# Turning the attention maps on VectorE and through DRAM instead of on TensorE, with a new order of TensorE's and GpSimd's work

## The chip, the cores and the metric

The kernel runs on one core of one Trainium2 chip. A core has TensorE (matrix products into the eight PSUM banks), VectorE, ScalarE and GpSimd, each with an instruction queue of its own that is worked through in the order in which it was written, and SyncE, which here only issues DMAs. GpSimd's queue issues DMAs too. The metric is the device time of one execution in microseconds (us); the median of three runs stands for a kernel.

## The reference

Two layers over 256 tokens of width 1024. In each layer the normalised input goes through one large projection, whose columns feed a gated DeltaNet branch and a differential attention branch. Cut to what the change touches:

```python
def attend(q_blk):                      # one head: two maps of 256 x 256
    s = jnp.einsum('nbhqd,nbhkd->nbhqk', q_blk, k).astype(f32)
    p = jax.nn.softmax(s, axis=-1)
    a = p[0] - lam * p[1]
    return jnp.einsum('bhqk,bhkd->bhqd', a.astype(v.dtype), v)
...
o = rmsnorm(o, subln_w) * (1.0 - lambda_init)
return o * jax.nn.silu(z)               # z: zb below
...
merged = (jax.nn.sigmoid(gate_a) * (y_a @ w_pa[l]) + jax.nn.sigmoid(gate_b) * (y_b @ w_pb[l]))
x = x + merged @ w_out[l]
```

There are eight heads of attention. The DeltaNet branch (the other eight heads) needs for each head and direction the inverse of a triangular matrix; the kernel inverts 32x32 blocks by substitution on VectorE and merges them into 64 and then 128 on TensorE.

## The kernel before

**Projections.** A projection of 512 columns contracts over 1024 rows in eight slices of 128 (`kt`). Each slice is six products on TensorE (two blocks of 128 tokens, three terms each, L324 to L326), since weights and activations are split into a high and a low part. I call these six products a step. Weights come in pairs of slices: SyncE loads `raw` (512 KB), ScalarE makes `hi` (L308), VectorE makes `lo = raw - hi` (L310). `hi` and `lo` have two buffers each, so a pair can be prepared only when TensorE is done with the pair two before it.

**Numbering.** From the projection `zb0` on, steps are counted from 0: `zb0` is 0 to 7, `zb1` 8 to 15, `za0` 16 to 23, `za1` 24 to 31, `gb0` 32 to 39, `gb1` 40 to 47, `ga0` 48 to 55, `ga1` 56 to 63, then `pb`. Everything else that TensorE does in this stage is put between steps.

**Attention, one head.** `scores` (L1053): four products `sc` per head (eight instructions in the trace, since a product of f32 is two), maxima on VectorE (`mx`, L1069), exponentials on ScalarE (`es`, L1071), the factor `cc` and the difference of the two maps on VectorE (L1074 to L1077). `turn` (L1081): four transposes `at` on TensorE into PSUM (L1088) and a copy to `aT` on ScalarE (L1090). `attend` (L1093): four products `av` with `vb` (L1099), a copy to `ob` and two sums of squares on ScalarE. The maps `es` and the turned maps `aT` have two buffers each.

**Inverse.** `substitute` (L865) runs 31 short pairs of VectorE instructions on `X` (L870, L871), spread over the projections until `za1`. `spread_blocks` (L873) copies `X` turned into `lt` and stores both to DRAM as `udr` on GpSimd's queue (L878). `merges` loads them back as `T` (L905; for the first group of heads by GpSimd's queue, for the second by SyncE's) and `U` (L909, GpSimd's queue), and then works in turns: `y64p` at step 41, `zt` at 43 and 45, `y128p` at 48, the next `zt` at 50. `weigh_q` needs products `kq` at 39, 42, 44 and 47. `chunks` follows from step 52 on.

**After attention.** The sums of squares `ssb` of all heads go to `rb` (VectorE, then a power on GpSimd, L155 and L156), `rb` scales `ob` (L1191, sixteen instructions), and `send` and `fetch` turn the result by the way that the change now uses for the maps: a transpose on VectorE inside blocks of 32x32 (L249), a store to DRAM on GpSimd's queue (L251), and four loads of 32 partitions each that put the blocks in their places (L257). The turned tile has its elements four apart in memory, and ScalarE and VectorE read it so (`split_B`, L263 and L265). The tiles `tb_v` of the DeltaNet branch go the same way (L135, L140, L142).

**What sets the order.** A scheduler orders the instructions of each engine by its own estimates; `behind(x)` (`tc.issue_after`) puts an instruction behind `x` in its engine's queue, and `keep_in_program_order` does so for the written order. Before the change only the first instructions of some groups are tied to a step (`place`); the rest is the scheduler's choice.

Of the kernel before, what the change touches and what calls it, by code (L numbers as in the profile page):

```python
# [17 lines left out]
P = 128  # L18
# [31 lines left out]
def hybrid_encoder(  # L50
# [53 lines left out]
    mark = {}  # L104
# [53 lines left out]
    def norm_row(w_row, nm):  # L158
# [14 lines left out]
        for i in range(3):  # L173
            mm = T.matmul(wb[i > 0], one if i else tri[:, 0, :], hl[:, i - 1] if i else row,
                          start=i < 2, stop=i != 1)
            tc.keep_in_program_order(mm)
# [138 lines left out]
    def proj_tm(act, w, c0, n, evac, nm, places=(None,) * 4, spare=(), later=None, turned=(), between=None,  # L315
# [3 lines left out]
        for kt, hi, lo in weights(w, c0, n, nm, places, later=later, spare=spare, turned=turned, held=held,  # L319
                                  first=first, raws=raws):  # L320
            for m in range(NM):
                ts_ = slice(m * P, (m + 1) * P)
                o = accs[m][:, :n]
                T.matmul(o, act[kt // 4][:, 0, kt % 4, ts_], hi, start=kt == 0, stop=False)  # L324
                T.matmul(o, act[kt // 4][:, 0, kt % 4, ts_], lo, start=False, stop=False)  # L325
                mark["proj"] = T.matmul(o, act[kt // 4][:, 1, kt % 4, ts_], hi, start=False,  # L326
                                        stop=kt == KT - 1).ins
                mark["done", nm, kt] = mark["proj"]
        if between:
            between()  # L330
        for m in range(NM):
            evac(m, accs[m][:, :n])
# [76 lines left out]
    for _ in range(5):  # L409
        mm = T.matmul(idle[:, :P], ones, ones, start=True, stop=True)  # L410
        tc.keep_in_program_order(mm)
# [22 lines left out]
    for m in range(NM):  # L434
        mm = T.matmul(pos_p[:, m : m + 1], pos_r[:, m * P : (m + 1) * P], ones[0:1, 0:1], start=True, stop=True)
        mark["pos"] = mm.ins
        tc.keep_in_program_order(mm)
# [69 lines left out]
    for l in range(DEPTH):  # L507
# [86 lines left out]
        def qk_part(s_, i):  # L594
                def evac_qk(m, ps):
# [11 lines left out]
                    for b in range(4):  # L607
# [4 lines left out]
                proj_tm(hT, wl, (C_QB, C_KB)[s_] + 512 * i, 512, evac_qk, f"qk{l}{s_}{i}",  # L612
                        turned=(0, 1) if (s_, i) == (0, 1) else ())
# [170 lines left out]
        def gram(nm, g, c, slot, after=None):  # L784
            gp = (bank if slot else bank_c)(f"{nm}{l}{g}{c}")
            for j4 in range(4):
                kqh = kq[:, 4 * g + j4, c]
                with behind(after):
                    mark[nm, g, c] = T.matmul(gp[:, j4 * P : (j4 + 1) * P], kqh[:, 0, :], kqh[:, slot, :],
                                              start=True, stop=True).ins  # L790
# [35 lines left out]
        def weigh_q(g, c, after):  # L826
            bv = B[:, c, 4 * g : 4 * g + 4]
            with tc.high_priority(offset=HP):
                gp = gram("kq", g, c, 1, after)
# [67 lines left out]
        def merges(g):  # L897
# [3 lines left out]
            G.memset(T64[blk(0), 0:8, 32:64], 0.0)  # L901
# [482 lines left out]
```

## Time and profile before

| | |
|---|---|
| time, median of three runs | 749.93 us (749.83 to 750.06) |
| span of the profiled execution | 748.5 us; the runs' median is 1.4 us longer, which lies around the span |
| busy | TensorE 739.3 us (99%), VectorE 586.5 (78%), ScalarE 481.2 (64%), GpSimd 139.5 (19%) |
| mean DMA rate | 181 GB/s |

A row of the groups gives line, engine, operation, output<-inputs, count, busy time and the mean of one in ns, then the idle time of the engine just ahead of it. A row of the timeline gives start, duration and what ran. Back to back instructions overlap in the trace, so what an instruction takes of its engine is read from start to start and not from its duration. "Issue" as a releaser means that nothing in the profile shows what was waited for.

### The profile page before, as it was taken

How to read it: one execution, taken by the hardware profiler on the slowest of the kernel's cores; microseconds unless marked ns; L12 is line 12 of the kernel's file. 1: busy time of each engine (PE TensorE's matmuls, PEld its weight loads, DVE VectorE, ACT ScalarE, POOL GpSimd, SP SyncE). 2: the span in 40 equal slices, each digit the busy share in tenths (PEclk: the TensorE clock that was granted, in tenths of full speed). 3: DMA queues.
4: the chain of work that ended last, by engine and by line, in shares of the span. 5: the costliest groups of instructions: out<-in, count | busy, mean ns of one | idle time of the engine just before them, and what ended most of it. 6: DMA issues, size and time to landing. Idle time of an engine off the chain costs nothing.

```text
span 748.5 us, 13917 instructions
## 1 busy us (share of the span) xinstructions
PE 739.3 (99%) x5176; PEld 641.7 (86%) x5176; DVE 586.5 (78%) x1109; ACT 481.2 (64%) x1022; POOL 139.5 (19%) x221
## 2 busy tenths in 40 slices
PE   8999999999999999999999999999999999999996
PEld 6999889987888889888889899889778888998885
DVE  8696898999985965578668779999999679537782
ACT  6757875667876576645456578555687757566552
POOL 6004110112023440100000150202110425301000
PEclk9999999999999999999999999999999999999999
DMA  8754566776667462567674466767666748335641
GB/s 260 239 170 169 170 179 198 209 211 193 208 177 186 145 184 84 171 200 247 199 232 133 128 192 180 219 176 230 195 171 195 197 133 229 95 114 201 220 141 57
DMA packets 73734, 135.46 MB, mean 181 GB/s; under 512 B 12944, under 2 KB 13921, under 8 KB 73666
## 3 DMA queue, kind: packets, MB, share of 16 engines
q1 hardware_dynamic: 64750, 113.65, 50.6%
q0 software_dynamic: 7936, 19.35, 8.7%
q10 hardware_dynamic: 980, 1.58, 0.6%
q8 instruction: 41, 0.67, 0.4%
q14 instruction: 27, 0.22, 0.1%
HBM read 125.53 MB, written 9.01 MB: 180 GB/s over the span
## 4 chain that ended last, share of the span: by engine, by line
PE 95%; ACT 2%; issue 1%; DVE 1%; DMA 1%; SPq 0%; POOLq 0%; POOL 0%; DVEq 0%; ACTq 0%
PE pp_vb L369 4%; PE pp_qk L325 4%; PE pp_qk L326 3%; PE pp_qk L324 3%; PE sc L1061 2%; PE pp_o L369 2%; PE pf_k L385 2%; PE pp_za L325 2%; PE pf_v L385 2%; PE pf_v L389 2%; PE pp_gb L324 2%; PE pp_gb L325 2%; PE pp_zb L324 2%; PE pf_q L387 2%; PE pf_k L387 2%; PE pf_v L387 2%
## 5 line engine op out<-in xcount | busy, mean ns | idle before, releaser
L325 PE MATMUL pp_qk<-lo_qk,hT 128*128 128x512 f32 x128 | 50.5, 395 | 0.3
L326 PE MATMUL pp_qk<-hi_qk,hT 128*128 128x512 f32 x128 | 50.0, 390 | 0.0
L310 DVE TENSOR_TENSOR lo_qk<-raw_qk,hi_qk 128x1024 fp32r<-128x1024 f32 x32 | 39.1, 1222 | 11.6 <-ACT hi_qk L308 11.4
L324 PE MATMUL pp_qk<-hi_qk,hT 128*128 128x512 f32 x128 | 45.1, 393 | 0.0
L308 ACT CAST hi_qk<-raw_qk 128x1024 fp32r<-128x1024 f32 x28 | 29.4, 1049 | 23.4 <-PE pp_qk L326 12.4
L1071 ACT ACTIVATE es<-sc,mx 128x256 f32<-128x256 f32 x64 | 29.6, 474 | 19.5 <-DVE mx L1069 19.5
L387 PE MATMUL pf_q<-hT,hi_q 128*128 128x256 f32 x128 | 36.1, 286 | 0.0
L385 PE MATMUL pf_k<-hT,hi_k 128*128 128x256 f32 x128 | 36.1, 287 | 0.0
L385 PE MATMUL pf_v<-hT,hi_v 128*128 128x256 f32 x128 | 35.9, 285 | 0.0
L387 PE MATMUL pf_v<-hT,hi_v 128*128 128x256 f32 x128 | 35.8, 284 | 0.0
L385 PE MATMUL pf_q<-hT,hi_q 128*128 128x256 f32 x128 | 35.8, 284 | 0.0
L387 PE MATMUL pf_k<-hT,hi_k 128*128 128x256 f32 x128 | 35.8, 284 | 0.0
L310 DVE TENSOR_TENSOR lo_pb<-raw_pb,hi_pb 128x1024 fp32r<-128x1024 f32 x16 | 19.6, 1225 | 20.5 <-ACT hi_pb L308 20.2
L389 PE MATMUL pf_q<-hT,lo_q 128*128 128x256 f32 x128 | 35.2, 288 | 0.0
L389 PE MATMUL pf_v<-hT,lo_v 128*128 128x256 f32 x128 | 34.6, 288 | 0.0
L389 PE MATMUL pf_k<-hT,lo_k 128*128 128x256 f32 x128 | 34.3, 284 | 0.0
L308 ACT CAST hi_pa<-raw_pa 128x1024 fp32r<-128x1024 f32 x16 | 16.8, 1053 | 22.3 <-PE pp_pa L326 16.1
L679 DVE SCALAR_TENSOR_TENSOR cvq<-pf_q,cw,cvq 128x254 f32<-128x254 f32 (+1 forms) x64 | 30.0, 479 | 0.9 <-ACT cvq L675 0.3
L679 DVE SCALAR_TENSOR_TENSOR cvv<-pf_v,cw,cvv 128x254 f32<-128x254 f32 (+1 forms) x64 | 30.1, 482 | 0.1
L679 DVE SCALAR_TENSOR_TENSOR cvk<-pf_k,cw,cvk 128x254 f32<-128x254 f32 (+1 forms) x64 | 29.0, 478 | 1.3 <-ACT cvk L675 0.6
L325 PEld LDWEIGHTS pp_qk<-lo_qk,hT 128*128 128x128 f32 x128 | 24.0, 188 | 6.6 <-DVE lo_qk L310 1.6
L310 DVE TENSOR_TENSOR lo_pa<-raw_pa,hi_pa 128x1024 fp32r<-128x1024 f32 x16 | 19.6, 1224 | 11.1 <-ACT hi_pa L308 11.1
(414 smaller groups left out, 2542.2 us busy)
## 6 DMA issues: line engine op xcount, KB each, us to landing
raw_qk<-in_w_in_dram SPq DMA_DIRECT2D x32, 512.0 KB, 3.8
raw_k<-in_w_in_dram SPq DMA_DIRECT2D x16, 512.0 KB, 4.7
raw_q<-in_w_in_dram SPq DMA_DIRECT2D x16, 512.0 KB, 3.7
raw_v<-in_w_in_dram SPq DMA_DIRECT2D x16, 512.0 KB, 3.8
raw_zb<-in_w_in_dram SPq DMA_DIRECT2D x16, 512.0 KB, 3.7
raw_za<-in_w_in_dram SPq DMA_DIRECT2D x16, 512.0 KB, 3.7
raw_ga<-in_w_in_dram SPq DMA_DIRECT2D x16, 512.0 KB, 4.4
raw_pb<-in_w_pb_dram SPq DMA_DIRECT2D x16, 512.0 KB, 3.8
```

The costliest lines, as they stand in the source:

```text
L308: high = (V.tensor_copy if kp in turned else S.copy)(hi[:, :, :n], raw[:, :, :n]).ins
L310: mark[nm, kp] = high, V.tensor_tensor(lo[:, :, :n], raw[:, :, :n], hi[:, :, :n].bitcast(F32), ALU.subtract).ins
L324: T.matmul(o, act[kt // 4][:, 0, kt % 4, ts_], hi, start=kt == 0, stop=False)
L325: T.matmul(o, act[kt // 4][:, 0, kt % 4, ts_], lo, start=False, stop=False)
L326: mark["proj"] = T.matmul(o, act[kt // 4][:, 1, kt % 4, ts_], hi, start=False, stop=kt == KT - 1).ins
L369: mark["proj"] = T.matmul(o, act[kt // 4][:, pa, kt % 4, ts_], ws[kt][1 + pw], start=kt == 0 and n_ == 0, stop=kt == KT - 1 and n_ == 2).ins
L385: T.matmul(o, hi[:, cs], act[kt // 4][:, 0, kt % 4, :], start=first, stop=False, skip_group_check=True)
L387: T.matmul(o, hi[:, cs], act[kt // 4][:, 1, kt % 4, :], start=False, stop=False, skip_group_check=True)
L389: T.matmul(o, lo[:, cs], act[kt // 4][:, 0, kt % 4, :], start=False, stop=done, skip_group_check=True)
L679: V.scalar_tensor_tensor(ca[:, o0:o1], acc[:, b, o0 + sft : o1 + sft], cw[:, j, cb : cb + 1], ca[:, o0:o1], ALU.mult, ALU.add)
L1061: mm = T.matmul(sp[n][:, qt * SEQ : (qt + 1) * SEQ], qkT[h // 4][rows, 0, h % 4, qt * P : (qt + 1) * P], qkT[h // 4][rows, 1, h % 4, :], s ...
L1071: S.activation(es[:, n, qt, :], spv[:, qt, :], AF.Exp, bias=mx[:, n, qt : qt + 1], accum_out=s_all[:, h, n, qt : qt + 1])
```

## The change

**TensorE's order is written out.** Each product of the projections, of attention and of the merges now goes through `mm`, which ties it behind the one before it. The chain begins at `zb0` and ends after `pb`. Projections became generators; `drive` takes a step and then runs the jobs that `plan` has put there.

**Places.** Scores come after steps 3, 8, 13, 18, 23, 28, 33, 37; the products with v after 14, 19, 24, 29, 34, 39, 44, 46. Before, scores began after 3, 7 and 12 and then every four steps, and the products with v followed some three steps later; the last were put after 39.

**Turning.** The four transposes on TensorE, the PSUM bank and ScalarE's copy go. VectorE transposes the blocks of the map into the free half of `es`, GpSimd's queue stores it as `att` and loads it back with four DMAs. The product reads its stationary operand with elements four apart (16 bytes).

**GpSimd's queue.** Loads of turned maps are kept in order by `mark["queued"]`. The clearing of `T` and its loads are tied behind the loads of head 5's map, the loads of `U` behind those of head 6's, and head 7's map behind `U`.

```diff
+    def mm(*args, **kw):
+        if mark["chain"] is None:
+            return T.matmul(*args, **kw)
+        with behind(mark["chain"]):
+            made = T.matmul(*args, **kw)
+        mark["chain"] = made.ins
+        return made
...
-            G.memset(T64[blk(0), 0:8, 32:64], 0.0)
-            G.memset(T64[blk(3), 8:16, 0:32], 0.0)
+            with behind(mark["queued"]):
+                G.memset(T64[blk(0), 0:8, 32:64], 0.0)
+                G.memset(T64[blk(3), 8:16, 0:32], 0.0)
             for b in range(4):
...
             for b in range(4 if g == 0 else 0):
-                G.dma_start(out=U_[blk(b), :, :, blk(b)].rearrange("j g t i -> j (g t) i"),
-                                  in_=udr[0, b].rearrange("g t j i -> j (g t) i"))
+                with behind(mark["queued"]):
+                    mark["queued"] = G.dma_start(out=U_[blk(b), :, :, blk(b)].rearrange("j g t i -> j (g t) i"),
+                                                 in_=udr[0, b].rearrange("g t j i -> j (g t) i")).ins
...
-                            mark["at", h] = T.transpose(ap_[:, kt * SEQ + qt * P : kt * SEQ + (qt + 1) * P],
-                                                        es[:, 0, qt, kt * P : (kt + 1) * P], ident).ins
-                S.copy(aT.rearrange("p k q -> p (k q)"), ap_)
...
+            V.transpose(es[:, 1].rearrange("p q k -> p (q k)").rearrange("p (b t x) -> p b x t", b=4, x=4),
+                        es[:, 0].rearrange("p q k -> p (q k)").rearrange("p (x b t) -> p b x t", b=4, x=4))
+            dd = dram.tile([4, 32, 4, P], F32, tag="att", name=f"att{l}{h}", bufs=4)
+            with behind(mark.get("queued")):
+                G.dma_start(out=dd.rearrange("i t j x -> (i t) (j x)"), in_=es[:, 1].rearrange("p q k -> p (q k)"))
+            back = work.tile([P, 4, 32, 4], F32, tag="w2a", name=f"aT{l}{h}", bufs=2)
+            for j in range(4):
+                with behind(mark.get("queued")):
+                    mark["queued"] = G.dma_start(out=back[blk(j)].rearrange("t i x k -> t i (x k)"),
+                                                 in_=dd[:, :, j].rearrange("i t x -> t i x")).ins
...
+            av = aT[h].rearrange("p i t x -> p x (i t)")
             for qt in range(NM):
                 for kt in range(NM):
...
+                    mm(op_[:, qt * P : (qt + 1) * P], av[:, 2 * qt + kt],
...
+        for h in range(NH):
+            plan((3, 8, 13, 18, 23, 28, 33, 37)[h], attention, h)
+        for h in range(NH):
+            plan((14, 19, 24, 29, 34, 39, 44, 46)[h], attend, h)
```

**What moves, on VectorE in `zb1`.** The rows stand between the difference of head 0's maps (`es`) and the low half of the third weight pair of `zb1`, steps 12 and 13 (`lo_zb_2210` before, `lo_zb_2211` after). Before:

```order
L1077 SCALAR_TENSOR_TENSOR es_2106<-es_2106,cc_2120 128x256 x2
L310 TENSOR_TENSOR lo_zb_2192<-raw_zb_2193,hi_zb_2191 128x1024
L1069 TENSOR_REDUCE mx_2126<-sc_2128 128x2
L399 SCALAR_TENSOR_TENSOR zb_0_385<-zb_0_385,pp_zb_2029 128x512
L1069 TENSOR_REDUCE mx_2126<-sc_2127 128x2
L871 TENSOR_TENSOR X_377<-X_377,fstmp_378 128x15x17
L690 SCALAR_TENSOR_TENSOR thv_1893<-thv_1893,cvv_1896 128x256
L310 TENSOR_TENSOR lo_zb_2210<-raw_zb_2211,hi_zb_2209 128x1024
```

The same piece of VectorE's queue after the change:

```order
L1074 SCALAR_TENSOR_TENSOR es_2066<-es_2066,cc_2080 128x256 x2
L321 TENSOR_TENSOR lo_zb_2193<-raw_zb_2194,hi_zb_2192 128x1024
L410 SCALAR_TENSOR_TENSOR zb_0_385<-zb_0_385,pp_zb_2029 128x512
L879 TENSOR_TENSOR X_377<-X_377,fstmp_378 128x15x17
L700 SCALAR_TENSOR_TENSOR thv_1893<-thv_1893,cvv_1896 128x256
L1082 STREAM_TRANSPOSE es_2066<-es_2066 128x4x4x32
L1066 TENSOR_REDUCE mx_2160<-sc_2162 128x2
L1066 TENSOR_REDUCE mx_2160<-sc_2161 128x2
L878 TENSOR_TENSOR fstmp_378<-la_375,X_377 128x256
L147 STREAM_TRANSPOSE tb_v_1904<-thv_1893 128x512
L321 TENSOR_TENSOR lo_zb_2211<-raw_zb_2212,hi_zb_2210 128x1024
```

The new transpose, a short instruction on `X` and the transpose of `tb_v` now stand ahead of that low half.

**What moves, on GpSimd's queue.** The rows run from the store of the inverted blocks (`udr`) to the loads of `T` and `U`. Before:

```order
L878 DMA udr_374<-X_377 8x8x1024 x2
L878 DMA udr_374<-lt_376 8x8x1024 x2
L909 DMA U__96<-udr_374 32x32x32 x4
L901 MEMSET T_2654 32x8x32
L902 MEMSET T_2654 32x8x32
L905 DMA T_2654<-udr_374 32x16x32 x4
```

After, with the maps of heads 5 and 6 (`att_2531` and `att_2649`) between them:

```order
L886 DMA udr_374<-X_377 8x8x1024 x2
L886 DMA udr_374<-lt_376 8x8x1024 x2
L1086 DMA att_2531<-es_2511 128x512
L1090 DMA aT_2533<-att_2531 32x4x128 x4
L910 MEMSET T_2591 32x8x32
L911 MEMSET T_2591 32x8x32
L915 DMA T_2591<-udr_374 32x16x32 x4
L910 MEMSET T_2598 32x8x32
L911 MEMSET T_2598 32x8x32
L1086 DMA att_2649<-es_2629 128x512
L1090 DMA aT_2651<-att_2649 32x4x128 x4
L920 DMA U__96<-udr_374 32x32x32 x4
```

`U` now stands behind two maps' ways through DRAM and behind `T`; just ahead of these rows stand the store and the loads of head 4's map, and head 7's follow.

**What moves, on VectorE ahead of `ga0`'s third weight pair.** That pair serves steps 52 and 53 (`lo_ga_2935` before, `lo_ga_3223` after). Before, half of the scaling of `ob` and its transposes is spread between the weight pairs ahead of it:

```order
L1233 SCALAR_TENSOR_TENSOR rb_2865<-rb_2865,r_2863 128x16
L1191 SCALAR_TENSOR_TENSOR ob_0_383<-ob_0_383,rb_2865,zb_0_385 128x128 x8
L249 STREAM_TRANSPOSE zb_0_385<-ob_0_383 128x4x4x32 x2
L830 TENSOR_TENSOR B_371<-kq_2849,B_371 128x1024
L310 TENSOR_TENSOR lo_ga_2899<-raw_ga_2900,hi_ga_2898 128x1024
L998 TENSOR_TENSOR ktm_360<-ktm_360,kds_372 128x512 x2
L1191 SCALAR_TENSOR_TENSOR ob_1_384<-ob_1_384,rb_2865,zb_1_386 128x128 x4
```

After, `rb` comes later, and all of the scaling stands in one piece ahead of the third pair:

```order
L321 TENSOR_TENSOR lo_ga_3145<-raw_ga_3146,hi_ga_3144 128x1024
L1000 TENSOR_TENSOR ktm_360<-ktm_360,kds_372 128x512 x2
L1233 SCALAR_TENSOR_TENSOR rb_3057<-rb_3057,r_3055 128x16
L1197 SCALAR_TENSOR_TENSOR ob_0_383<-ob_0_383,rb_3057,zb_0_385 128x128 x8
L147 STREAM_TRANSPOSE tb_q_3200<-kq_359 128x512
L1197 SCALAR_TENSOR_TENSOR ob_1_384<-ob_1_384,rb_3057,zb_1_386 128x128 x8
L260 STREAM_TRANSPOSE zb_0_385<-ob_0_383 128x4x4x32 x2
L321 TENSOR_TENSOR lo_ga_3223<-raw_ga_3224,hi_ga_3222 128x1024
```

The third pair's low half now follows `rb`, and through it the last product with v, which moved from step 39 to step 46.

More of the change, by code (lines that the diff above doesn't have):

```diff
@@ L313, in weights, with proj_tm @@
                 yield 2 * kp + k, hi[:, k, :n], lo[:, k, :n]
[L315 removed]
+    def proj_tm(act, w, c0, n, evac, nm, places=(None,) * 4, spare=(), later=None, turned=(),
                 banks=None, held=None, first=(), raws={}):
@@ L1279, in hybrid_encoder @@
             gated(osb, za, ro, nw[:, 0:1], yaT, f"ya{l}", (m,))
-        branch(yaT, w_pa[l], gta, f"pa{l}")
+        for i in range(2):
+            full(branch(yaT, w_pa[l], gta, f"pa{l}", i))
         mT = pair(f"mT{l}")
```

262 lines of the change are left out of this document (120 added, 142 removed).

## Prediction, made before the changed kernel ran

> **What bounds the kernel now.** I read the busy shares first, then the chain that ended last, then the stretches of the stage that changes, then its timeline engine by engine.
>
> ```profile
> PE 739.3 (99%) x5176; PEld 641.7 (86%) x5176; DVE 586.5 (78%) x1109; ACT 481.2 (64%) x1022; POOL 139.5 (19%) x221
> PE 95%; ACT 2%; issue 1%; DVE 1%; DMA 1%; SPq 0%; POOLq 0%; POOL 0%; DVEq 0%; ACTq 0%
> core 0: us, PE busy (x) PEld busy (x) DVE busy (x) ACT busy (x) POOL busy (x), PEclk, DMA share, GB/s
> 158.00:214.00 56.00, 56.00 (x296) 44.63 (x295) 54.04 (x121) 43.31 (x116) 6.41 (x12) 1.00 0.63 187
> 214.00:262.00 48.00, 48.00 (x607) 39.93 (x606) 36.33 (x61) 30.56 (x73) 17.56 (x28) 1.00 0.63 177
> 524.00:580.00 56.00, 56.00 (x296) 44.64 (x295) 54.02 (x121) 43.33 (x116) 6.45 (x12) 1.00 0.63 187
> ```
>
> TensorE is the bound: 95% of the chain is its own work, so an instruction less on it is time, if nothing else arrives late. The stretches say where something may. In layer 0 the first six heads of attention lie in 158 to 214 us, and there VectorE is busy for 54.04 of 56.00 us; layer 1 (524 to 580) has the same picture. VectorE has 2 us to spare just where the change gives it more work. After 214 it has 12 of 48 us.
>
> **What goes.** Here is TensorE around the transposes of one head, with the products of a projection behind:
>
> ```profile
> 199.99 0.60 PE L1088 MATMUL at<-ident,es 128*128 128x128 f32 x4
> 200.51 1.13 PE L1061 MATMUL sc<-qkT 64*128 64x256 f32 x8
> 202.61 0.39 PE L324 MATMUL pp_za<-hi_za,hT 128*128 128x512 f32 x1
> 202.84 0.39 PE L325 MATMUL pp_za<-lo_za,hT 128*128 128x512 f32 x1
> ...
> 205.26 0.48 PE L325 MATMUL pp_za<-lo_za,hT 128*128 128x512 f32 x1
> 205.57 0.40 PE L326 MATMUL pp_za<-hi_za,hT 128*128 128x512 f32 x1
> L1090 ACT COPY aT<-at 128x512 f32<-128x512 f32 x16 | 9.4, 585 | 0.0
> ```
>
> Four transposes take 200.51 - 199.99 = 0.52 us. Eight heads: 4.2 us a layer. The written order also has about three places fewer at which TensorE goes from f32 back to a projection, and the first product there takes 205.57 - 205.26 = 0.31 us instead of 0.23, so some 0.1 us each: 0.3 us. **Term A: -4.5 us a layer.** ScalarE's 16 copies (9.4 us) go too; ScalarE is at 43 of 56 us in the tight stretch and TensorE does not wait for it there, so I count them at nothing. A projection's product takes 0.23 us from start to start (202.61 to 202.84), so a step is 1.37 us.
>
> **What comes.** The transpose on VectorE is like `send`'s, and the way through DRAM like that of `tb_v`:
>
> ```profile
> 247.87 2.01 DVE L249 STREAM_TRANSPOSE zb<-ob 128x512 f32<-128x512 f32 x2
> 249.72 1.21 DVE L830 TENSOR_TENSOR B<-kq,B 128x1024 f32<-128x1024 f32 x1
> 180.50 0.71 DVE L135 STREAM_TRANSPOSE tb_v<-thv 128x512 f32<-128x512 f32 x1
> 181.50 0.56 POOL L140 DMA_DIRECT2D bnc_v<-tb_v  x1 [8.44 <-DVE tb_v L135]
> 185.33 2.17 POOL L142 DMA_DIRECT2D tb_v<-bnc_v  x4 [3.26 <-issue]
> DMA to landing us min/median/max: 2.1/3.3/5.7
> ```
>
> A transpose takes (249.72 - 247.87) / 2 = 0.93 us of VectorE. The store starts 0.3 us after the transpose ends (181.21 to 181.50), the loads 3.8 us after the store; the last of the four starts 1.6 us later and lands after 3.3, the median of this way's DMAs. So a map is there 0.3 + 3.8 + 1.6 + 3.3 = 9.0 us after its transpose.
>
> **Term B: head 0 to the merges.** Head 0 first. Up to the row at 175.35 VectorE's queue is the same as before.
>
> ```profile
> 172.66 1.06 PE sc L1061 x8
> 175.35 1.24 DVE L310 TENSOR_TENSOR lo_zb<-raw_zb,hi_zb 128x1024 fp32r<-128x1024 f32 x1
> 177.09 0.70 DVE L399 SCALAR_TENSOR_TENSOR zb<-zb,pp_zb 128x512 f32<-128x512 f32 x1
> 178.28 0.44 DVE L871 TENSOR_TENSOR X<-X,fstmp 128x255 f32<-128x255 f32 x1
> 178.62 0.44 DVE L690 SCALAR_TENSOR_TENSOR thv<-thv,cvv 128x256 f32<-128x256 f32 x1
> ```
>
> From 175.35 the new queue has `lo` (1.14 from start to start), the `zb` product (0.60), `X` (0.34), `thv` (0.33) and then the transpose: it ends at 178.7. Plus 9.0 gives 187.7 for the map. TensorE's old start of head 1's scores is 172.66; the new order puts them one step later (174.0), then come 1.1 us of scores, steps 9 to 13, head 2's scores and step 14: 174.0 + 1.1 + 6 x 1.37 + 1.1 + 0.3 for the changes of kind = 184.7. TensorE would wait 3.0 us at step 14, part of it already at step 12, whose low half now stands behind two transposes and two maxima. Two more low halves stand behind a map's transpose (steps 18 and 22, where no transposes of TensorE fill the time any more), up to 0.93 each: 1.9. Sum 4.9.
>
> A second way to the same lateness goes by GpSimd's queue to `U`, needed at step 43:
>
> ```profile
> 205.12 0.88 DVE L1077 SCALAR_TENSOR_TENSOR es<-es,cc 128x256 f32<-128x256 f32 x2
> 213.05 1.27 POOL L878 DMA_DIRECT2D udr<-X  x2 [25.55 <-issue]
> 222.79 3.15 POOL L909 DMA_DIRECT2D U__96<-udr  x4 [7.37 <-issue]
> 226.57 2.57 POOL L905 DMA_DIRECT2D T<-udr  x4
> 245.59 0.72 PE L937 MATMUL zt<-U__96,y 32*32 32x32 f32 x62
> ```
>
> Head 4's map was ready at 206.0; with five transposes ahead on a full engine it is turned at 206.0 + 5 x 0.93 = 210.7. Store and loads: 0.3 + 3.8 + 2.2, so `udr` is stored from 217.0 instead of 213.05. Its landing took 222.79 - 213.05 = 9.7 us: 226.7. Then `T` (2.6) with the clearing ahead of it (0.6, from the end of `U`'s row to `T`'s start), head 6's map (3.8 + 2.2), `U` (3.15, landing after 4.1 by its median): 226.7 + 3.2 + 6.0 + 2.4 + 4.1 = 242.4. TensorE without any wait would reach `zt` at 245.59 - 4.5 - 2 x 0.89 (two products with v that come later) = 239.3. Lateness 3.1. The two ways are not added: the first delays TensorE, and `U` is then in time. Bounds for B: 3.1, the second way alone, and 6.9 (VectorE's 2 us of idle time left as they are, on top of 4.9). I take **B: +4.9 us a layer**, near the first way.
>
> **Term C: `ga0`'s third weight pair (step 52).** The new queue has all of `ob`'s scaling ahead of it, and `rb` waits for head 7.
>
> ```profile
> 242.69 0.89 PE kq L789 x8
> 240.10 1.46 PE L923 MATMUL y64p<-T,A 32*32 32x32 f32 x128
> 245.55 0.18 DVE L1233 SCALAR_TENSOR_TENSOR rb<-rb,r 128x16 f32<-128x16 f32 x1 [0.71 <-POOL rb L156]
> 245.76 2.19 DVE L1191 SCALAR_TENSOR_TENSOR ob<-ob,rb,zb 128x128 f32<-128x128 f32 x8
> 257.27 2.13 PE L960 MATMUL y128p<-T,A 64*64 64x64 f32 x64
> L1207 ACT ACTIVATE gb<-pp_gb 128x512 f32<-128x512 f32 x8 | 4.8, 596 | 0.1
> ```
>
> Before, head 7's product ended at about 240.1 (`y64p` follows it) and `rb` ran at 245.55, 5.4 us later. From there now: 0.2, eight scalings 2.1, a transpose of `tb_q` 0.6 (adjacent elements, as in `tb_v`'s row less the overlap), eight more 2.1, two transposes 1.9, the low half 1.2, and 0.6 for a `gb` evacuation that ScalarE has between: 14.1. TensorE goes from head 7 (step 46) to step 52's second product through five steps (6.8), `kq` 0.9, `y128p` and `zt`, as many instructions, 2.1 each, and 0.6 besides: 12.5. **C: +1.6 us a layer**; bounds 0, if the pieces overlap, and 3.
>
> **Sum.** -4.5 + 4.9 + 1.6 = +2.0 a layer, +4.0 for both. The span of 748.5 becomes 752.5; the runs' median of 749.93 lies 1.4 above the span: 753.9.
>
> **The unknown price: a strided stationary operand.** The product with v reads `aT` with elements 16 bytes apart. No TensorE instruction of before does. ScalarE does:
>
> ```profile
> L263 ACT ACTIVATE ybT<-zb,nw 128x512 fp32r<-128x512 f32 x8 | 9.9, 1241 | 0.0
> L244 ACT ACTIVATE yaT<-pt_ya,nw 128x512 fp32r<-128x512 f32 x8 | 5.1, 682 | 0.0
> L1088 PEld LDWEIGHTS at<-ident,es x64: 138/139/146, 176.7 to 598.5; 128*128 128x128 f32 x64
> L1099 PEld LDWEIGHTS av<-vb,aT x128: 187/192/193, 179.9 to 605.5; 128*128 128x128 f32 x128
> 196.52 0.89 PE av L1099 x8
> ```
>
> The same operation takes 1241 instead of 682 ns with its input four elements apart: 1.09 ns more an element. On 128 columns that is 0.14 us a load, and with the 128 loads of the `av` row 17.9 us. The other bound is 0. I take 0, because TensorE loads 128 columns of `at` in 139 ns and those of `av` in 192 (minimum, median and maximum are given): the load of `av` is not limited by how fast a column can be read, which leaves a stride 0.05 us of slack, and the 0.11 us of the product before (0.89 us for eight) run beside it. Together that is more than 0.14.
>
> [...]
>
> **The rivals.**
>
> *Strided loads are dear.* Term D of up to +17.9, half of it if the load hides in part. Delays of the first six products also give `U` and the low halves time, so I take 12: 753.9 + 12 = 766. For it: ScalarE's rows. Against: the slack and the overlap.
>
> *TensorE's waits are hidden.* This one ends faster. Its place is VectorE between step 9 and the store of `udr`. The 2 us of idle time there and a landing at the minimum (2.1 instead of 3.3) cover 3.2 of B's 4.9, and C falls to 0. With B at 1.7: -2.8 a layer, 749.9 - 5.6 = 744. It decides where B and C together fall below 4.5. Against it: the queue's order is fixed, and 3.0 of B comes from a sum in which VectorE never waits. With nothing late at all the time would be 749.9 - 9.0 = 741.
>
> *A draw.* B and C equal A within 0.7 us a layer: 748.5 to 751.4.
>
> *The change does not do what it says*: the order of TensorE's queue shows the transposes gone and the places as written, so I give this no chance.
>
> **How the numbers follow.** Forecast (waits of 5 to 11 us a layer, cheap loads) 0.50, from 751.5 to 762; strided loads dear 0.17 (760 to 772); hidden 0.23 (741 to 748.4); draw 0.10. The range leaves out 0.1 on either side: 743 to 767. About 0.2%, 1.5 us, is what a measurement can tell from no change: faster 0.23, same 0.12 (the draw and the forecast's lower edge), slower 0.65.
>
> **What would show it.** Right: the groups have no L1088; the stretch from 158 us on shows VectorE above 95%; `av` of head 0 shows TensorE idle for about 3 us until a load of `aT`; the pair at steps 52 and 53 has TensorE waiting for `lo_ga`. Wrong: TensorE without idle time there (B, C), or the 16 groups of `av` longer than 0.89 us each (D). A landing far from 3.3 us, or `att` held behind `udr` in the queue, would upset B the most.

## The result and the profile after

The changed kernel takes **780.96 us** (778.67 to 782.83) against 749.93: a ratio of 1.041, with the 95% interval 1.0389 to 1.043. The profiled execution has a span of 781.1 us (before 748.5), so there are 32.6 us to explain. The forecast had 4.0.

Busy shares and the chain of the changed kernel:

```profile
PE 754.6 (97%) x5112; PEld 651.6 (83%) x5112; DVE 603.0 (77%) x1125; ACT 475.2 (61%) x1006; POOL 183.2 (23%) x301
PE 56%; DVE 5%; issue 3%; DMA 2%; ACT 1%; POOL 0%; POOLq 0%; DVEq 0%; ACTq 0%
```

TensorE runs 64 instructions less than before and is busy 15.3 us longer: the work that stayed became slower. And it is no longer busy throughout, so it also waits. (How much, the chain can't say: its shares add up to 67%, so it wasn't followed through a third of the span.) First the waits of TensorE (who, for what, us in total, times, longest); before, this view had nothing of this stage:

```profile
PE pp_zb L110 <- DVE lo_zb L321: 4.0, 2, 2.0
PE pp_ga L110 <- DVE lo_ga L321: 3.0, 2, 1.5
PE zt L110 <- DMA U__96<-udr: 2.9, 1, 2.9
PE av L110 <- issue: 2.7, 1, 2.7
PE pp_za L110 <- DVE lo_za L321: 2.7, 3, 1.0
PE av L110 <- DMA aT<-att: 2.6, 1, 2.6
```

They sum to 17.9 us, nearly all at places that the forecast named: low halves behind a map's transpose, the first product with v, `U`, and `ga0`'s third pair. Only the low half of step 28 (0.83 us in each layer, two of the three waits for `lo_za`) is not among them. The second source is in TensorE's timeline (start, duration, what; in brackets what it waited for):

```profile
179.37 0.61 PE L110 MATMUL pp_zb<-hi_zb,hT 128*128 128x512 f32 x2
181.99 0.50 PE L110 MATMUL pp_zb<-lo_zb,hT 128*128 128x512 f32 x1 [2.00 <-DVE lo_zb L321]
...
187.03 0.39 PE L110 MATMUL pp_zb<-hi_zb,hT 128*128 128x512 f32 x1
190.15 2.10 PE L110 MATMUL av<-vb,aT 128*128 128x128 f32 x8 [2.73 <-issue]
192.01 0.65 PE L110 MATMUL pp_zb<-hi_zb,hT 128*128 128x512 f32 x1
192.46 0.63 PE L110 MATMUL pp_zb<-lo_zb,hT 128*128 128x512 f32 x1
192.89 1.05 PE L110 MATMUL pp_zb<-hi_zb,hT 128*128 128x512 f32 x2
...
201.91 1.91 PE L110 MATMUL av<-vb,aT 128*128 128x128 f32 x8
203.57 0.48 PE L110 MATMUL pp_za<-hi_za,hT 128*128 128x512 f32 x1
```

Head 1's eight products, which wait for nothing, take 203.57 - 201.91 = 1.66 us. Their loads in the view of the tile `av` (minimum, median and maximum in ns; before 187/192/193):

```profile
L110 PEld LDWEIGHTS av<-vb,aT x128: 308/329/332, 190.1 to 649.6; 128*128 128x128 f32 x128
```

A third source shows in the same rows: from 192.46 to 192.89 one product of a projection takes 0.43 us instead of 0.23. The stretches of 3.41 us around it have the granted clock in the column behind the five engines, with the DMA share next to it:

```profile
188.74:192.16 3.42, 2.01 (x9) 2.04 (x10) 1.82 (x6) 0.68 (x4) 0.11 (x1) 1.00 0.80 261
192.16:195.57 3.41, 3.41 (x10) 2.63 (x10) 1.95 (x6) 2.88 (x9) 2.07 (x4) 0.50 0.27 78
195.57:198.98 3.41, 3.41 (x16) 2.68 (x15) 3.24 (x5) 3.24 (x9) 0.56 (x1) 1.00 0.15 49
257.01:263.84 6.83, 6.27 (x107) 5.63 (x108) 0.00 (x0) 2.25 (x6) 2.18 (x4) 0.50 0.18 53
```

Behind its three longest waits, those of 2.6 to 2.9 us, TensorE runs at half clock for one or two such stretches; behind the two of 2.0 us it does not. Besides the two stretches shown there is 577.86 to 581.28, behind layer 1's wait for head 0's map: 13.65 us in all, of which at most half, 6.8, is lost.

### The profile page after: what moved, and what is told of

The parts are those of the page before. It is cut to its first block, busy times and chain, and to the rows that moved or that the text cites. A ratio compares the mean times of both kernels' runs of the same rounds, so it can differ in the third digit from the quotient of the medians.

```text
span 781.1 us, 13961 instructions
## 1 busy us (share of the span) xinstructions
PE 754.6 (97%) x5112; PEld 651.6 (83%) x5112; DVE 603.0 (77%) x1125; ACT 475.2 (61%) x1006; POOL 183.2 (23%) x301
## 4 chain that ended last, share of the span: by engine, by line
PE 56%; DVE 5%; issue 3%; DMA 2%; ACT 1%; POOL 0%; POOLq 0%; DVEq 0%; ACTq 0%
PE pp_pb L110 6%; PE pp_pa L108 6%; PE pp_ga L110 4%; PE pp_gb L110 4%; PE pp_qk L108 4%; PE pp_vb L380 3%; PE pp_o L108 3%; PE pp_za L110 2%; PE av L110 2%; PE pp_o L380 2%; PE po L110 2%; DVE ob L1197 1%; PE pf_k L396 1%; PE pf_v L396 1%; PE pf_v L400 1%
## 5 line engine op out<-in xcount | busy, mean ns | idle before, releaser
L108 PEld LDWEIGHTS pp_qk<-hi_qk,hT 128*128 128x128 f32 x256 | 47.4, 188 | 9.1
L321 DVE TENSOR_TENSOR lo_qk<-raw_qk,hi_qk 128x1024 fp32r<-128x1024 f32 x32 | 39.1, 1221 | 10.9 <-ACT hi_qk L319 10.6
L1090 POOL DMA_DIRECT2D aT<-att x64 | 35.1, 556 | 52.4 <-PE sc L110 10.0
L110 PE MATMUL pp_ga<-hi_ga,hT 128*128 128x512 f32 x128 | 45.8, 408 | 0.0
L110 PE MATMUL pp_za<-hi_za,hT 128*128 128x512 f32 x128 | 43.8, 405 | 0.0
L110 PE MATMUL pp_zb<-hi_zb,hT 128*128 128x512 f32 x128 | 43.7, 410 | 0.0
L110 PE MATMUL pp_pb<-hi_pb,ybT 128*128 128x512 f32 x128 | 42.7, 399 | 0.0
L110 PE MATMUL pp_gb<-hi_gb,hT 128*128 128x512 f32 x112 | 40.2, 414 | 0.0
L108 PE MATMUL pp_pa<-hi_pa,yaT 128*128 128x512 f32 x128 | 39.8, 389 | 0.0
L110 PEld LDWEIGHTS av<-vb,aT 128*128 128x128 f32 x128 | 31.2, 325 | 6.8 <-issue 6.1
L110 PE MATMUL av<-vb,aT 128*128 128x128 f32 x128 | 31.0, 387 | 5.3 <-issue 2.7
```

The source lines that it names most:

```text
L108: return T.matmul(*args, **kw)
L110: made = T.matmul(*args, **kw)
L321: mark[nm, kp] = high, V.tensor_tensor(lo[:, :, :n], raw[:, :, :n], hi[:, :, :n].bitcast(F32), ALU.subtract).ins
L1090: mark["queued"] = G.dma_start(out=back[blk(j)].rearrange("t i x k -> t i (x k)"), in_=dd[:, :, j].rearrange("i t x -> t i x")).ins
```

## The experiments

Each changes the changed kernel, unless it says that it changes the kernel before; none leaves work out. Ratios are to the kernel before, run on the same chip.

### The step of 16 bytes alone

The kernel before, with one edit: ScalarE's copy writes `aT` with elements four apart, and the product reads it so. Order and ways stay.

```diff
-                S.copy(aT.rearrange("p k q -> p (k q)"), ap_)
+                S.copy(aT.rearrange("p k q -> p (k q)").rearrange("p (t x) -> p x t", x=4),
+                       ap_.rearrange("p (x t) -> p x t", x=4))
...
-                            T.matmul(op_[...], aT[:, kt, qt * P : (qt + 1) * P],
+                            T.matmul(op_[...], aT.rearrange("p k q -> p (k q)").rearrange("p (t x) -> p x t", x=4)[:, 2 * kt + qt],
```

> The kernel before, its order unchanged, but ScalarE's copy writes the turned map with elements 16 bytes apart and the product with v reads it so. Theory A, the step costs TensorE 325 - 192 = 133 ns a load, of which the product before hides a little, as in the changed kernel: 0.77 us for eight, 12.3 us in all, 762 us, and no waits. Theory B, in the changed kernel the loads were slow because transfers or VectorE used the same memory at that time: here they stay at 192 ns and the time is 750 us.

Measured: 763.80 us (763.4 to 763.85), ratio 1.0179 (1.0164 to 1.0194): +13.6 us over 750.24. The loads of `av` and one group of eight in the timeline:

```profile
L1100 PEld LDWEIGHTS av<-vb,aT x128: 308/329/332, 179.4 to 618.6; 128*128 128x128 f32 x128
```

```profile
197.56 1.91 PE L1100 MATMUL av<-vb,aT 128*128 128x128 f32 x8
199.22 0.48 PE L325 MATMUL pp_za<-lo_za,hT 128*128 128x512 f32 x1
```

The loads show the changed kernel's 329 ns, no wait of this stage appears, and the eight products take 1.66 us (before 0.81, from 196.35 to 197.16). 0.85 x 16 groups = 13.6, which is the whole difference. A load grew by 329 - 192 = 137 ns and each product by 0.85 / 8 = 106 ns, so some 30 ns of a load's growth are hidden and the rest is on TensorE's path.

**How far apart is too far?** The same edit with 8 bytes instead of 16 (`"p (k t x) -> p k x t", k=2, x=2`, and the product reads two apart):

> As e3_step_alone, but with elements 8 bytes apart in place of 16. Theory A, a load pays for each 16 bytes that it touches: 8 bytes apart costs half of what 16 does or nothing, a load of 192 to 260 ns and 750 to 757 us. Theory B, any step other than adjacent costs the whole: 329 ns and 763.8 us.

```profile
L1100 PEld LDWEIGHTS av<-vb,aT x128: 193/196/198, 180.0 to 606.5; 128*128 128x128 f32 x128
```

Measured: 751.20 us (750.69 to 752.76), ratio 1.0015 (1.0006 to 1.0024), +0.9. With elements 8 bytes apart the load is back at 196 ns.

### The order alone

The changed kernel's order, with the transposes and ScalarE's copy back on TensorE and ScalarE (after steps 12, 17, 22, 27, 32, 36, 43 and 45), no way through DRAM, and `T` and `U` not tied.

```diff
+            ap_ = bank(f"at{l}{h}")
+            back = work.tile([P, 4, P], F32, tag="w2a", name=f"aT{l}{h}", bufs=2)
...
+                        mark["chain"] = T.transpose(ap_[:, (2 * qt + kt) * P : (2 * qt + kt + 1) * P], es[:, 0, qt, kt * P : (kt + 1) * P], ident).ins
+            S.copy(back.rearrange("p x q -> p (x q)"), ap_)
...
+            plan((12, 17, 22, 27, 32, 36, 43, 45)[h], lambda h: turn(h, es[h]), h)
```

> The changed kernel's order of TensorE (scores at steps 3, 8, 13 and so on, products with v at 14, 19 and so on, merges and chunks as they stand), but the maps turned by TensorE and copied by ScalarE as before the change, one or two steps ahead of the product with v; no transpose on VectorE, no store, no map loads, and nothing to tie GpSimd's queue behind. Theory A, the waits come from VectorE's transposes and the way through DRAM: no wait for a map or for `U`, loads of 192 ns, and with some 0.1 us a head for one more change of kind the time is 750 to 753 us. Theory B, the new order by itself brings the waits for low halves and for `ob`'s scaling: 1 to 2 us each at steps 12, 18, 22 and 52, 755 to 762 us.

Measured: 759.59 us (758.85 to 761.15), ratio 1.0126 (1.0109 to 1.0143). Its waits:

```profile
PE pp_ga L110 <- DVE lo_ga L321: 3.0, 2, 1.5
PE pp_zb L110 <- DVE lo_zb L321: 2.2, 2, 1.1
PE pp_za L110 <- DVE lo_za L321: 0.6, 2, 0.3
```

The order is dear without any way through DRAM: the span is 9.0 longer than before's, 5.8 of it waits. The other 3.2 are not idle time. They can't all be charged to the changed kernel's order: the transposes stand at places of their own here, so that from `zb0` to `pb` TensorE leaves the projections 47 times a layer (40 before, 41 in the changed kernel). The wait for `lo_zb` fell from 2.0 to 1.1 each: 0.9 of it was the map's block transpose; the rest is left with the short instruction on `X` and `tb_v`'s transpose (0.97 us together, 179.13 to 180.10), which the order alone puts ahead of that low half.

### The waits, one at a time

**Head 0's and head 1's products with v later**, after steps 17 and 21 instead of 14 and 19, since a map lands 11.4 us after its transpose:

```diff
-            plan((14, 19, 24, 29, 34, 39, 44, 46)[h], attend, h)
+            plan((17, 21, 24, 29, 34, 39, 44, 46)[h], attend, h)
```

> The changed kernel with the products with v of heads 0 and 1 at steps 17 and 21 in place of 14 and 19; nothing else is moved. Theory A, the waits of 2.7 and 2.6 us of head 0's product are the time that a map needs through DRAM, and the stretches of half clock behind them (3.4 us from 192.16 and from 577.86) follow from these waits: both waits and both stretches go, 5.3 us and about 2 x 1.7 us, 772 to 773 us. Theory B, VectorE is the bound there: TensorE runs into the low halves of steps 14 to 22 that much earlier and waits for them instead, and the time is 776 to 781 us.

Measured: 770.20 us (767.86 to 771.96), ratio 1.026 (1.0243 to 1.0278). The waits at `av` and those for `lo_za` are gone and the one at `U` falls to 1.6, which leaves 8.6 us of waits: 9.3 less, and the span is 10.9 shorter. The half clock did not go (the granted clock over the span is 0.991, in the changed kernel 0.990); in layer 0 it moved behind the wait of 2.0 us for `lo_zb`, at which the changed kernel kept its full clock. First this run, then the changed kernel at the same wait:

```profile
179.77:183.19 3.42, 1.42 (x7) 1.13 (x7) 3.42 (x6) 3.42 (x11) 1.51 (x4) 1.00 0.55 170
183.19:186.60 3.41, 3.41 (x11) 2.29 (x11) 3.32 (x9) 0.80 (x2) 3.41 (x7) 0.50 0.90 275
```

```profile
178.50:181.92 3.42, 1.49 (x7) 0.91 (x5) 3.42 (x7) 2.60 (x9) 1.12 (x2) 1.00 0.53 199
181.92:185.33 3.41, 3.34 (x17) 2.57 (x19) 3.41 (x11) 1.96 (x6) 2.73 (x5) 1.00 0.89 258
```

The bounds of these stretches run on in steps of 3.41 us. Here the whole wait lay within one of them (1.42 us busy, 2.00 idle); in the changed kernel all but 0.07 us of it did (1.49 busy, 1.93 idle), and the clock held.

**`U` first.** `T` and `U` ahead of the store and loads of head 5's map, whose product moves from 39 to 42:

```diff
+            if h != 5:
+                send_map(h)
...
+        plan(32, step, mg)
+        plan(32, send_map, 5)
```

> The changed kernel with head 5's store and loads put behind the loads of `T` and `U` in GpSimd's queue in place of ahead of them, and its product with v at step 42 in place of 39. Theory A, `U` is late in layer 0 (2.86 us, and 6.8 us of half clock around it) because head 5's loads wait for a buffer that head 3's product with v frees at 235.6, and hold the queue: the wait for `U` and that half clock go, 5 to 6 us, 775 to 776 us. Theory B, `U` is late because `udr` is stored and lands late: TensorE still waits 2 us or more for `U` or `T`, or now for head 5's map, and the time is 779 to 783 us.

Measured: 778.16 us (777.74 to 778.76), ratio 1.0378 (1.0362 to 1.0393). The wait at `zt` is gone and the granted clock is 0.994 instead of 0.990, as the theory that GpSimd's queue holds `U` says. But 5 to 6 us were to go and 2.8 went (4.8 in the spans): the waits for `lo_za` grew from 2.7 to 4.0 and those for `lo_zb` from 4.0 to 4.4. What held the queue in the changed kernel shows in GpSimd's timeline:

```profile
229.60 0.61 POOL L1086 DMA_DIRECT2D att<-es  x1 [2.44 <-DVE za L410]
235.87 2.20 POOL L1090 DMA_DIRECT2D aT<-att  x4 [5.67 <-PE av L110]
...
249.25 2.34 POOL L920 DMA_DIRECT2D U__96<-udr  x3 [1.17 <-issue]
```

Head 5's loads need the `aT` buffer of head 3, which is free only after that head's product (step 29). They stand 5.67 us at the head of the queue, and everything for `T` and `U` stands behind them.

**Less on VectorE.** Three low halves to GpSimd:

```diff
-                    mark[nm, kp] = high, V.tensor_tensor(lo[:, :, :n], raw[:, :, :n],
+                    mark[nm, kp] = high, (G if (nm[:2] + nm[3:], kp) in (("zb1", 2), ("za0", 3), ("za1", 2)) else V).tensor_tensor(lo[:, :, :n], raw[:, :, :n],
```

> The changed kernel with the low halves of three weight pairs a layer (zb1's third, za0's fourth, za1's third: those that TensorE waited 2.0, 1.0 and 0.8 us for) made by GpSimd in place of VectorE. Theory A, VectorE has too much to do from 160 to 215 us, some 3.6 us a layer: with 3 x 1.14 us less the waits for low halves fall from 3.9 us in layer 0 and 2.8 in layer 1 to under 1 each, and 775 to 777 us follow if the wait for the first map stays. Theory B, a subtraction on GpSimd takes well over 2 us and slows VectorE beside it, and GpSimd's queue is held from its stores: the waits stay or grow, 780 to 788 us.

Measured: 790.80 us (787.06 to 794.14), ratio 1.0544 (1.0509 to 1.058): worse. GpSimd's timeline:

```profile
180.06 2.38 POOL L321 TENSOR_TENSOR lo_zb<-raw_zb,hi_zb 128x1024 fp32r<-128x1024 f32 x1 [5.33 <-ACT hi_zb L319]
182.39 0.58 POOL L1086 DMA_DIRECT2D att<-es  x1
```

The store of head 0's map starts at 182.39 instead of 179.35. The waits for low halves fell from 6.7 to 4.3 us, those at `av` rose from 5.3 to 16.0 (9.8 for `aT`, 6.2 for `tb_v`). So GpSimd, whose queue issues the maps' DMAs, was no free engine here.

### Both causes, taken away together

**The order mended, the step kept.** Scores of head 1 one step earlier, VectorE's transposes of heads 0 to 4 each tied behind a low half, products with v at 20, 23, 26, 30, 36, 42, 44 and 46, `T` and `U` ahead of head 5's loads, and the second half of `ob`'s scaling behind `ga0`'s third low half.

```diff
+            with behind(mark[low[h][0], low[h][1]][1] if h in low else None):
+              V.transpose(es[:, 1]...
...
+        low = {0: (f"zb{l}1", 2), 1: (f"zb{l}1", 3), 2: (f"za{l}0", 1), 3: (f"za{l}0", 3), 4: (f"za{l}1", 2)}
+            plan((12, 14, 18, 22, 28, 32, 36, 39)[h], lambda h: turn(h, es[h]), h)
+            plan((20, 23, 26, 30, 36, 42, 44, 46)[h], attend, h)
...
+            at = [mark[f"ga{l}0", 2][1] if i else mark[f"gb{l}1", 2 + m][1] for m in range(NM)]
```

> As e7_all, but the map keeps the changed kernel's way: one store of 256 KB, four loads with runs of 512 bytes, and the product with v reads elements 16 bytes apart; head 5's store may run ahead of `U`, the last two scores stand at 33 and 37. Theory A, e7_all was late only because its stores in runs of 128 bytes and its single load take 5 to 6 us each to land: here the waits for maps and low halves are under 3 us in all, no half clock follows, and what is left beside the kernel before is the step (+13.7), the transposes (-7.2) and some changes of kind (+2): 757 to 760 us. Theory B, VectorE's surplus shows up whatever the way of the map: 10 us of waits or more, 766 to 775 us.

Measured: 763.94 us (762.96 to 765.86), ratio 1.0186 (1.0172 to 1.02). What is left of waits in this stage:

```profile
PE av L110 <- DMA aT<-att: 2.6, 3, 1.4
PE pp_za L110 <- DVE lo_za L321: 1.9, 2, 0.9
PE pp_zb L110 <- DVE lo_zb L321: 0.9, 2, 0.6
...
PE pp_zb L110 <- DVE cvv L689: 0.6, 1, 0.6
```

No wait is over 1.4 us, and no stretch of this stage has half clock (the granted clock is 1.00 from 158 to 214 us and from 524 to 580, and 0.999 over the span). 17.0 us came back with the order alone, and what remains is the time of the kernel before with nothing but the step (763.80; in spans 764.1 against 761.7). So what the change saves on TensorE is spent by the 6.0 us of waits that are left, and the step comes on top.

**The step taken away too.** VectorE transposes into adjacent places; a map then goes by four stores with runs of 512 bytes, instead of one store with runs of 2 KB, and by four loads with runs of 128 instead of 512 bytes. First with the changed kernel's order:

```diff
-            dd = dram.tile([4, 32, 4, P], F32, tag="att", name=f"att{l}{h}", bufs=4)
+            dd = dram.tile([4, 4, 32, P], F32, tag="att", name=f"att{l}{h}", bufs=4)
+            for i in range(4):
...
+                    G.dma_start(out=dd[i].rearrange("j t x -> t j x"), in_=es[blk(i), 1]...)
...
+                    mark["queued"] = G.dma_start(out=back[:, :, i], in_=dd[i].rearrange("j t (x r) -> (j t) x r", x=4)).ins
-            av = aT[h].rearrange("p i t x -> p x (i t)")
+            av = aT[h].rearrange("p x i r -> p x (i r)")
```

> The changed kernel, but the map comes back with each stationary block's 128 elements side by side: VectorE writes its blocks adjacent, four stores of 64 KB in place of one of 256 KB, and the four loads write runs of 128 bytes. Theory A, the step of 16 bytes is what made the load of `av` 325 ns: the loads go back to 192 ns, eight products to 0.89 us, and with 16 heads 16 x 0.77 = 12.3 us go; the longer way through DRAM (three more issues of 0.55 us, 1.6 us a map) gives some of it back where TensorE waits for a map: up to 2 x 1.6 and a few us of half clock. 769 to 777 us. Theory B, the load is slow because the operand was written by a transfer and not by ScalarE: `av` stays at 1.66 us, and the time at 781 to 788.

Measured: 778.07 us (776.37 to 780.2), ratio 1.0372 (1.035 to 1.0394). The step's cost is gone (loads at 192 ns), but only 2.9 us of 13.6 came back:

```profile
PE av L110 <- DMA aT<-att: 7.3, 3, 3.0
PE zt L110 <- DMA U__96<-udr: 5.2, 2, 4.6
```

TensorE arrives earlier, the maps do not, and GpSimd has 48 DMAs more to issue: the waits are 21.4 us in all instead of 17.9, and the granted clock is 0.986 instead of 0.990.

Then with the mended order, and in a second form with four stores of 128-byte runs and one load:

> As e8_all_step_kept, but with e1_adjacent's way of the map (four stores with runs of 512 bytes, four loads that write runs of 128 bytes), so that the elements lie side by side. Theory A, with the order mended and maps landing as in e1_adjacent (3 to 4 us for each half of the way) nothing is late by more than 3 us in all: 744 to 749 us, below the kernel before. Theory B, the three more issues a map on GpSimd's queue make maps or `U` late again: 752 to 765 us.

> The changed kernel with every cause found so far taken away at once: the map comes back with its stationary elements side by side (four stores with runs of 128 bytes, one load with runs of 2 KB, so no step of 16 bytes); the block transposes of heads 0 to 4 put behind the low half that TensorE waited for (zb1's third and fourth, za0's second and fourth, za1's third), head 1's scores at step 7, the last two at 32 and 36; products with v at steps 20, 23, 26, 30, 36, 42, 44, 46; the loads of `T` and `U` ahead of head 5's map; the scaling of `ob`'s second half behind ga0's third low half. Theory A, these are the causes, and nothing is late behind them: 781 less 13.7 for the step, 17.9 for the waits and about 6 for the half clock is 743 us, and with up to 2.5 us for changes of kind 743 to 747, less than before the change. Theory B, VectorE's surplus of 3.6 us a layer before 215 us does not go away by order alone: low halves or maps are late at other steps, 4 to 8 us a layer with half clock behind the longer ones, 752 to 760 us.

Measured: 777.11 us (776.24 to 779.22), ratio 1.0365 (1.0351 to 1.0379), and for the one load 782.65 us (779.81 to 783.8), ratio 1.0417 (1.0396 to 1.0439). Neither came where a theory had it. The new wait of the first, 12.6 us for `aT` in two times some 6.3, has its cause in GpSimd's queue:

```profile
209.08 2.19 POOL L1088 DMA_DIRECT2D att<-es  x4 [1.46 <-DVE fstmp L878]
217.40 1.72 POOL L886 DMA_DIRECT2D udr<-X  x2 [6.13 <-issue]
219.97 0.82 POOL L1099 DMA_DIRECT2D aT<-att  x1 [0.85 <-issue]
```

The store of `udr` stands between the store and the loads of head 3's map and waits for the inverse, and the loads wait with it. In the second form the DMAs land late (launches, KB each, median us to landing; the changed kernel has 2.6 for `att` and 3.7 for `aT`):

```profile
att<-es POOLq DMA_DIRECT2D x64, 64.0 KB, 5.1
aT<-att POOLq DMA_DIRECT2D x16, 256.0 KB, 6.0
```

### Two tries at something faster

**8 bytes, mended order, `udr` behind head 4's loads.** The transpose leaves pairs (`g=2, x=2`), the product reads two apart, and the early products come one or two steps later.

```diff
+                    with behind(mark["queued"]):
+                     mark["udr"] = G.dma_start(out=udr[w, ...
...
+            back = work.tile([P, 2, 4, 32, 2], F32, tag="w2a", name=f"aT{l}{h}", bufs=2)
+            av = aT[h].rearrange("p g i r x -> p g x (i r)")
```

> As e10_all_adjacent, with three edits: the map lies with elements 8 bytes apart (e9_step_8: nearly free), so that the four loads write runs of 256 bytes in place of 128; the stores of `udr` stand behind head 4's loads in GpSimd's queue (in e10_all_adjacent they held head 3's loads until the inverse was ready, and TensorE waited 6.2 us); products with v of heads 0 to 3 at steps 21, 25, 28 and 32. Theory A, that place in the queue and the first maps' lateness were all that was left: waits under 4 us in all, no half clock, and 744 to 750 us. Theory B, four stores and four loads a map are too much for GpSimd's queue: a map or `U` is late by 2 us or more with half clock behind it, and the time is 754 to 765 us.

Measured: 768.66 us (765.49 to 770.99), ratio 1.0244 (1.0218 to 1.0269). Loads take 196 ns and `av` waits 1.3 us in all. The waits moved on: 5.1 us at scores for exponentials that stand in ScalarE's queue behind a later piece of `za`, and 2.4 at `y64p` for `T`. Behind layer 0's wait at scores (2.54 us) the clock is at one half from 203.92 to 210.74, and over the span it is 0.987.

**Only heads 0 to 4 by VectorE and DRAM**, heads 5 to 7 by TensorE after steps 34, 38 and 42; the five maps lie 8 bytes apart (one store, eight loads each), and `udr` stays behind head 4's loads:

```diff
+            plan((12, 14, 18, 22, 28, 34, 38, 42)[h], lambda h: (turn if h < 5 else turn_on_pe)(h, es[h]), h)
```

> As e8_all_step_kept, but only the maps of heads 0 to 4 go by VectorE and DRAM; those of heads 5 to 7 are turned by TensorE at steps 34, 38 and 42 (products with v at 35, 39 and 43), so that GpSimd's queue is free for `T` and `U`. The five maps lie with elements 8 bytes apart (one store, eight loads with runs of 256 bytes), their products with v stand at steps 20, 25, 29, 33 and 37, and `udr` is stored behind head 4's loads. Theory A, the terms add up: five heads' transposes gone (5 x 0.45 us a layer, 4.5 us), no step, some 0.2 us for each change of kind that the order has more (2 to 3 us), and waits of 2 to 4 us for low halves: 748 to 752 us, level with the kernel before. Theory B, a map through DRAM makes something late whatever its place: waits over 8 us with half clock behind them, 757 us or more.

Measured: 771.34 us (768.7 to 773.58), ratio 1.0277 (1.0252 to 1.0301). Its largest wait:

```profile
PE y64p L110 <- DMA T<-udr: 5.0, 2, 4.7
```

Tied behind head 4's loads, `udr` is stored at 228.33 instead of 224.91, and `T` is late. No version beat the kernel before. A third buffer for `aT` and loads of `T` and `U` on another queue were not tried.

## Why the prediction was right and wrong

The sign was right, and so were the places where TensorE waits. The size was not. In spans, the 32.6 us divide into

| | forecast, both layers | measured | from |
|---|---|---|---|
| D, strided loads | 0 (bound 17.9) | +13.2 | span of the step alone, 761.7 - 748.5 |
| B and C, waits | +13.0 | +17.9 | the waits view |
| A, transposes and changes of kind | -9.0 | -3.6 | mended order: 764.1 - 748.5 - 13.2 - 6.0 |
| half clock | none | +5.1 | the rest of 32.6; at most 6.8 by the stretches |

The spans are of single executions, and the executions of one such kernel differ by 3 to 4 us; the two remainders, A and half clock, are good to about 2 us. By medians A would be 763.94 - 763.80 - 6.0 = -5.9, still short of -9.0.

- **The step that failed is D's**: "which leaves a stride 0.05 us of slack, and the 0.11 us of the product before run beside it. Together that is more than 0.14." The price itself, taken over from another engine, was right: ScalarE's rows had given 0.14 us, and the load grew by 137 ns. It was the cover that was not there. Of the 0.05 us of slack nothing showed, since the load grew by the full price. Of the 0.11 us beside the product before, 0.03 showed: eight products went from 0.81 to 1.66 us, 0.106 us more for each of the eight, and 128 of these are the 13.6 us measured. The bound of 17.9, which the text gave and then set aside, was nearer than the value it took. The loads took 329 ns at 16 bytes apart, 196 at 8 and 192 adjacent. That the loads pay stood in the text as the rival "strided loads are dear" at 766; it came, and the forecast's waits came with it.
- **A was too large.** The transposes took 7.2 us start to start over both layers (0.45 a head, not 0.52). The text counted three places fewer a layer at which TensorE goes back to a projection; the traces have 40 before, 41 in the changed kernel and 40 in the mended order. And two costs were in no term. Scores make the product ahead of them longer (199.01 to 199.34 below: 0.33 us instead of 0.23; the first behind, 0.34, cost as much before). Sixteen groups of scores now stand directly behind a product of a projection, and before only six, the others standing behind transposes: ten more, some 1.0 us.

```profile
199.01 0.40 PE L110 MATMUL pp_za<-hi_za,hT 128*128 128x512 f32 x1
199.34 1.14 PE L110 MATMUL sc<-qkT 64*128 64x256 f32 x8
200.40 0.50 PE L110 MATMUL pp_za<-hi_za,hT 128*128 128x512 f32 x1
200.74 0.39 PE L110 MATMUL pp_za<-lo_za,hT 128*128 128x512 f32 x1
```

  A wait also costs more than the waits view counts. The product ahead of it runs to its end (0.39 us from 187.03), and the first behind it takes 0.34 (181.99 to 182.33), both instead of 0.23: some 0.27 us a wait, 2.2 for the eight waits of the mended order. -7.2 + 1.0 + 2.2 = -4.0 is near the -3.6 of the table. This is an estimate from the traces; no run takes these costs apart.
- **B was right in mechanism and too small.** VectorE's queue went as worked out:

```profile
177.71 1.09 DVE L1082 STREAM_TRANSPOSE es<-es 128x512 f32<-128x512 f32 x1
178.65 1.24 DVE L1066 TENSOR_REDUCE mx<-sc 128x2 f32<-128x512 f32 x2
...
180.12 0.71 DVE L147 STREAM_TRANSPOSE tb_v<-thv 128x512 f32<-128x512 f32 x1
180.74 1.19 DVE L321 TENSOR_TENSOR lo_zb<-raw_zb,hi_zb 128x1024 fp32r<-128x1024 f32 x1
```

  The transpose ends at 178.8 (178.7 forecast). The map took 11.4 us from there, not 9.0, to the row at 190.15: the store starts 0.55 later, the loads 3.2 after it, and the last of them needs some 6 us, with the DMAs 89 to 100% busy from 181.92 to 188.74. The low half at step 12 cost 2.0 us, which the text had only as part of step 14's wait. Both together took 4.73 in layer 0; the text had 3.0. (Of the low halves at steps 18 and 22, forecast at 1.9 a layer, only that of step 22 in layer 0 was waited for, 1.0 us; step 28, which the text did not name, took 0.8 in each layer.) "The two ways are not added" was wrong in layer 0: the wait for `U` (2.9) came on top, because the queue was held by head 5's loads for a buffer, which the text did not see.
- **C was right**: 1.5 us in each layer, against 1.6.
- **Half clock was in no term.** It stands behind the longer waits, those of 2.6 to 2.9 us: the mended order, whose waits are at most 1.4, has none, and with the wait at `av` gone it moved to a wait of 2.00 us that had none before.
- Of the signs named ahead, `av` above 0.89 us did say D, and the idle time at step 14 and at steps 52 and 53 did say B and C. VectorE above 95% from 158 us on did not come: it was busy for 50.6 of 56 us, since TensorE's waits stretch the same work over more time.

Where the expected gain went is therefore shown by three kernels: the step alone costs 13.6 us, the order with the transposes kept 9.3, and the kernel with its order mended is level with the one that has the step alone. That half clock takes 5.1 rests on the balance and on the bound of the stretches.

## What to carry to other kernels

When TensorE is the bound, look at how far apart a stationary operand's elements lie when the transpose is done. Here a load took 192 ns with adjacent elements, 196 with elements 8 bytes apart and 329 with 16: measure the load and charge its growth to every product (106 of 137 ns came through here), not less a hoped-for overlap. Price a way through DRAM by all that stands in its issuing queue, including a load that waits for a buffer (5.67 us here), and by its landing at the DMA share of that moment (0.89 to 1.00 where the map took 11.4 us). And a wait costs more than itself where the clock drops behind it: here it did behind waits of 2.6 to 2.9 us and behind one of 2.00, not behind another of 2.00 nor behind those of up to 1.4 us in the mended order.

## What the hardware showed beside

- The clock was halved in steps of 3.41 us with bounds that run on evenly: from 192.16 to 257.01 are 19 steps, to 577.86 are 113. A stretch with 2.00 us idle and 1.42 busy (the 179.77 row above) was followed by half clock; one with 1.93 idle and 1.49 busy (the 178.50 row) was not, nor was the one at the same wait of layer 1 (564.21 in the changed kernel, 1.55 busy). Two others ahead of half clock were busy for 1.11 us (253.60, changed kernel) and 1.37 us (200.50, 8 bytes with the mended order). A stretch can be busier and still be followed by half clock: the one at 188.74, with strided products, was busy for 2.01 us; the one at 185.33, with scores and 2.09 us, was not followed by it. None of the stretches named here was idle throughout.
- VectorE's block transpose of the same 128x512 map took 1.10 us where it wrote elements 16 bytes apart and 0.71 where it wrote them adjacent. The row below is of the kernel with adjacent maps (median 708 ns).

```profile
L1082 DVE STREAM_TRANSPOSE es<-es x16: 695/708/715, 177.8 to 619.8; 128x512 f32<-128x512 f32 x16
```

- GpSimd took 2.38 us for a subtraction (`lo_zb`, 128x1024) that took VectorE 1.21 us on average in the changed kernel.
